# A transformer of two layers with routed experts: the last normalization's rows loaded behind the second nest, and a sixth further weight slot in that layer

## The chip, the core and the metric

The kernel runs on one core of a Trainium2 chip, as one launch. The metric is device microseconds of an execution, as the median of several runs. The profile is of one further execution, with its own time.

## What is computed

256 tokens of width 1024 go through two layers. Layer 0 mixes tokens by attention (with a context of 256 further tokens), layer 1 by a gated long convolution. Behind each mixer stands a normalization, a mixture of 16 experts of which each token takes two, and another normalization. Cut to what matters here:

```
for i in range(2):
    y = attention(...) if i == 0 else hyena(...)
    x = layer_norm(alpha * x + g1 * y, ln_g[i, 0], ln_b[i, 0])
    f = moe_ffn(x * (1 + sc2) + sh2, router_w, router_bias, exp_w_gate[i], exp_w_up[i], exp_w_down[i])
    x = layer_norm(alpha * x + g2 * f, ln_g[i, 1], ln_b[i, 1])
return x
```

`moe_ffn` computes `(silu(t @ w_gate[e]) * (t @ w_up[e])) @ w_down[e]` for each token `t` and each of its two experts `e`, weighted by the router. All is float32. One expert's three matrices are 12 MB, which the kernel loads as 12 tiles of 1 MB: four gate, four up, four down.

## The kernel before

**Weights and slots.** All weights go through tiles named `w` of 128 x 2048 float32 (1 MB), loaded by SP in the order of the program (line 144, in `load`). `ring` has 12 of them (`RING`). In the experts of a layer, `more_ring` opens further slots beside the ring, named w0, w1 and so on: four in layer 0 and five in layer 1 (`MORE = [4, 5]`). `wtile` hands the slots out by turns: the ring's 12, then the further ones, then the ring's again. A load into a slot waits until the last reader of what was in it has ended. SP issues strictly in order, so a load that waits holds up all loads behind it.

**The experts of a layer** are in `moe`. The experts are sorted by their number of tokens and taken by position. Positions 0 to 9 are always computed in blocks of 32 tokens or 64: `up` (line 646, the gate and up products), `turn_mid` (line 655), `down` (line 665), `back` (lines 684 and 690, which adds into `xs`). The two fullest experts are computed densely over all 256 tokens, in eight pieces, one in each of the positions 1 to 8 (`PIECES`): an up piece (`dense_up`, line 709) or a down piece (`dense_down`, line 721), each with four or two of the 1 MB tiles. Positions 10 and up are rarely needed. They stand in a nest of branches (`rare`, line 759), which is entered only if such a position has tokens.

**Around the nest.** Position 9 (`NEST`) is computed behind the nest, but its first loads are issued ahead of it, into the further slots alone: `expert_loads(l, ix, most=MORE[l], new=True)`. `new=True` takes w0, w1 and so on from the start. To this end position 8's down tiles are kept to the ring (`all_slots(0)`). Behind the nest come the rest of position 9's loads:

```
w = expert_loads(l, ix, most=MORE[l], new=True)
last.back()
last = None
rare(RARE)
E.bank = E.banks()
E.w = expert_loads(l, ix, have=w)
```

**The end.** Behind layer 1's experts the last normalization is computed by DVE (`ln_stats`, lines 359 to 365, then lines 1407 and 1408), with `ln_g[1, 1]` and `ln_b[1, 1]` spread over all partitions in a tile `gbf` of 1 MB. `gbf` lies in a pool `gp` of its own, and POOL loads it (line 1399). The order in which each engine's instructions stand is set by a scheduler when the program is built: `gbf`'s loads stand far ahead of the experts, at the start of layer 1's mixer. The result leaves by lines 1410 and 1412.

Two tiles of the dense experts matter to the change: `hid` (128 x 1024, one buffer), which holds the hidden values of a dense piece, and `do` (128 x 512, two buffers), which takes its scaled output (line 723). Both are free once position 8's dense down piece is done, unless the innermost branch of the nest (`beyond`) uses them.

Of the kernel before, what the change touches and what calls it, by code (L numbers as in the profile page):

```python
# [7 lines left out]
F32 = mybir.dt.float32  # L8
# [4 lines left out]
ALU = mybir.AluOpType  # L13
# [5 lines left out]
N, D, NE, FF = 256, 1024, 16, 1024  # L19
# [6 lines left out]
PAD = -3e38  # L26
RING = 12

MORE = [4, 5]


DENSE = 2
# [45 lines left out]
def emit(tc, I, O):  # L78
    nc = tc.nc
    pe, act, dve, pool, sp = nc.tensor, nc.scalar, nc.vector, nc.gpsimd, nc.sync  # L80
    es = ExitStack()

    with es:
# [42 lines left out]
        def all_slots(n):  # L126
            slots["more"] = n
            slots["turn"] = RING + n - 1
# [49 lines left out]
        xs = cp.tile([128, 2, D], F32, name="xs")  # L178
# [169 lines left out]
        def row_bc(pool_, src, tag, eng):  # L348
            t = pool_.tile([128, D], F32, name=tag, tag=tag, bufs=1)
            eng.dma_start(out=t, in_=src.to_broadcast([128, D]))  # L350
            return t

        def mod_bc(pool_, l, v, tag, eng):
            return row_bc(pool_, mdram[l, v].rearrange("a b -> (a b)")[None, :], tag, eng)

        def ln_stats(r, e=0):
            st = sm.tile([128, 2, 6], F32, name="st")
            for hf in range(2):
                dve.bn_stats(st[:, hf, :], r[:, 512 * hf:512 * hf + 512])  # L359
            mv = sm.tile([128, 2], F32, name="mv")  # L360
            dve.bn_aggr(mv, st)  # L361
            sd = sm.tile([128, 1], F32, name="sd")
            act.activation(sd, mv[:, 1:2], AF.Sqrt, bias=epsc[:, e:e + 1])
            rs = sm.tile([128, 1], F32, name="rs")
            dve.reciprocal(rs, sd)  # L365
            return mv, rs
# [37 lines left out]
        def mixer_tail(l, stage, mixT, wout, R):  # L404

            g1b = mod_bc(stage, l, 0, "g1b", sp)
            early = expert_loads(l, 0, most=MORE[l], new=True)
            all_slots(MORE[l])
            ca, cb = fold[:, l, 0], fold[:, l, 1]
# [315 lines left out]

        ENG = [ET.PE, ET.Activation, ET.DVE, ET.Pool, ET.SP]

        def moe(l, h2, R, first, filler):
            with tc.tile_pool(name=f"mp{l}", bufs=2, reuse_waits="tile") as mp:
                g2b = mod_bc(mp, l, 1, "g2b", pool)  # L730
                g2r = mp.tile([128, 256], F32, name="g2r", tag="g2r", bufs=1)
# [7 lines left out]
                def expert(p):  # L739
                    i = place(p)  # L740
                    tab = (R["rank"][:, :, 0:1], R["wt"][:, :, 0:1]) if p == 0 else (R["rankP"][:, :, i:i + 1], R["wtP"][:, :, i:i + 1])
                    return Expert(mp, SLOTS[i], tab, h2, (fold[:, l, 0], fold[:, l, 1]), (g2b, g2r), p == NEST)
# [1 line left out]
                def number(row, i, engines, top):  # L744
                    return nc.values_load(ints[0:1, row, i:i + 1], engines=engines, min_val=0, max_val=top)

                lng = row_bc(mp, I["ln_g"][l, 0:1, :], "hid", pool)
                lnb = [mp.tile([128, 512], F32, name="do", tag="do", bufs=2) for _ in range(2)]
                for hf in range(2):
                    pool.dma_start(out=lnb[hf], in_=I["ln_b"][l, 0:1, 512 * hf:512 * hf + 512].to_broadcast([128, 512]))  # L750
                E = expert(0)
                E.pick(R["weights"])
                with tc.issue_after(E.turn_in()):
                    R["permute"](mp)
                second = expert_loads(l, 1, most=MORE[l])
                def rare(p):


                    with tc.If(number(4, place(p), ENG, N + 1) > 0):  # L759
                        E = expert(p)  # L760
                        E.w = expert_loads(l, number(1, place(p), [ET.SP], NE - 1))
                        E.pick()
                        E.turn_in()
                        E.up()
                        E.weights_in()
                        E.turn_mid()
                        E.down()
                        E.back()
                        if p + 1 < NPOS:
                            rare(p + 1)  # L770
                        else:
                            with tc.If(number(2, 0, ENG, 1) > 0):
                                beyond()
# [28 lines left out]
                hid, last = {}, None  # L802
                for p in range(RARE):
                    if p == NEST:

                        ix = number(1, place(p), [ET.SP], NE - 1)
                        w = expert_loads(l, ix, most=MORE[l], new=True)
                        last.back()
                        last = None
                        rare(RARE)  # L810
                        E.bank = E.banks()
                        E.w = expert_loads(l, ix, have=w)
                    elif p == 0:
                        E.w = first
                    else:
                        ix = number(1, place(p), [ET.SP], NE - 1) if p > 1 else 1
                        E.w = expert_loads(l, ix, have=second if p == 1 else (), most=8)
                        if p in PIECES:
                            r, half, down = PIECES[p]
                            dw = dense_loads(l, number(1, 2 + r, [ET.SP], NE - 1), half, down)  # L820
                        if p + 1 == NEST:
                            all_slots(0)
                        E.w = expert_loads(l, ix, have=E.w)
                    E.up()
                    if last:
                        last.back()
                    nxt = expert(p + 1) if p + 1 < RARE else None
                    if nxt:
                        nxt.pick()
                    if p == 0:  # L830
                        for t in range(2):
                            dve.tensor_tensor(out=xs[:, t, :], in0=h2[:, t, :], in1=lng, op=ALU.mult)
                            for hf in range(2):
                                s_ = slice(512 * hf, 512 * hf + 512)
                                dve.tensor_tensor(out=xs[:, t, s_], in0=xs[:, t, s_], in1=lnb[hf], op=ALU.add)
                    E.turn_mid()
                    if p in PIECES:
                        if down:
                            dense_down(mp, E.bank, dw, hid[r], R["wtP"][:, :, 2 + r:3 + r], g2b)
                        else:  # L840
                            hid[r] = dense_up(mp, E.bank, dw, h2T)
                    if filler:
                        filler(p, E.bank)
                    if nxt:
                        nxt.turn_in()
                    if p != NEST:
                        E.weights_in()
                    E.down()
                    if p + 1 == NEST:
                        nxt.weights_in()  # L850
                    E, last = nxt, E
                last.back()

                act.activation(dumm, epsc[:, 0:1], AF.Sqrt)
                if l == 0:
                    for t in range(2):
                        ln_core(xs[:, t, :], xs[:, t, :], 1)
# [15 lines left out]
        R = routing_tables()  # L873
        mixT = hm([128, KC, N], "mixT")
        with tc.tile_pool(name="s0", bufs=1) as s0:
# [15 lines left out]
            for h in mod_first():  # L891
# [3 lines left out]
                for dc in range(4 * h, 4 * h + 4):  # L895
                    for r in range(2):
# [3 lines left out]
                        else:  # L900
                            dve.tensor_scalar(out=v_, in0=v_, scalar1=scp[:, r, dc:dc + 1], scalar2=mcol(0, 0, r)[:, dc:dc + 1],
                                              op0=ALU.mult, op1=ALU.add)
# [183 lines left out]
            mv = [c_ for l in range(2) for v in range(6) if l or v > 1 for c_ in mod_vec(l, v)]  # L1086
# [30 lines left out]
            for qc in range(2):  # L1117
                sq = tmp()
                pool.tensor_tensor(out=sq, in0=o_sb[:, qc].rearrange("p h d -> p (h d)"),
                                   in1=o_sb[:, qc].rearrange("p h d -> p (h d)"), op=ALU.mult)  # L1120
# [14 lines left out]
        if True:  # L1135
            wo = out_weights(I["attn_w_out"][0])
            rmore = more_ring(0)
            with tc.tile_pool(name="s0b", bufs=1, reuse_waits="tile") as s0b:
                h2, first = mixer_tail(0, s0b, mixT, wo, R)
# [105 lines left out]
        R = routing_tables()  # L1245
        if True:
# [146 lines left out]
            rmore = more_ring(1)  # L1393
            with tc.tile_pool(name="s1b", bufs=1, reuse_waits="tile") as s1b:
                h2, first = mixer_tail(1, s1b, z2T, wo, R)
        gp = es.enter_context(tc.tile_pool(name="gp", bufs=1, reuse_waits="tile", side="right"))
        gbf = gp.tile([128, 2, D], F32, name="gbf")
        for a, nm in enumerate(("ln_g", "ln_b")):
            pool.dma_start(out=gbf[:, a], in_=I[nm][1, 1:2, :].to_broadcast([128, D]))
        moe(1, h2, R, first, None)  # L1400
        ov = O["out"].rearrange("o (t p) d -> p (o t) d", p=128)
        st = [ln_stats(xs[:, t, :], 1) for t in range(2)]
        for t in range(2):
            mv, rs = st[t]
            for hf in range(2):
                s_ = slice(512 * hf, 512 * hf + 512)
                dve.scalar_tensor_tensor(out=xs[:, t, s_], in0=xs[:, t, s_], scalar=mv[:, 0:1], in1=gbf[:, 0, s_], op0=ALU.subtract, op1=ALU.mult)  # L1407
                dve.scalar_tensor_tensor(out=xs[:, t, s_], in0=xs[:, t, s_], scalar=rs, in1=gbf[:, 1, s_], op0=ALU.mult, op1=ALU.add)  # L1408
                if t:
                    (act if hf else sp).dma_start(out=ov[:, t, s_], in_=xs[:, t, s_])  # L1410
            if t == 0:
                sp.dma_start(out=ov[:, t, :], in_=xs[:, t, :])
        less_ring(rmore)


# [57 lines left out]
```

## Time and profile before

| | us |
|---|---|
| median of 3 runs | 1301.54 |
| lowest and highest of them | 1300.76, 1306.81 |
| the profiled execution | 1297.5 |
| its span, first to last instruction | 1295.7 |
| TensorE (PE) busy | 1161.9, 90% of the span |
| VectorE (DVE) busy | 549.3, 42% |
| ScalarE (ACT) busy | 214.9, 17% |
| GpSimd (POOL) busy | 48.8, 4% |
| DMA | 443.87 MB, mean 343 GB/s |
| mean granted TensorE clock | 0.953 of full speed |

Times in the profile are from the span's start. PE is TensorE's matmuls, PEld its weight loads, PEq its sequencer, SPq the instruction stream of SP that issues loads. DMA share is the mean busy share of the core's 16 DMA engines. A float32 matmul stands in the trace as two records. The two nests end at about 720 us (layer 0, whose nest is taken) and 1257 us (layer 1, whose nest is not taken).

### The profile page before, as it was taken

Reading aid. Unit: us, or ns where it says so; the run is one execution under the profiler, and the core shown is the slowest. Engines: PE = TensorE matmul, PEld = TensorE weight load, DVE = VectorE, ACT = ScalarE, POOL = GpSimd, SP = SyncE. Lnnn points to the kernel's source line nnn. Section 1 sums busy time; section 2 is a strip of 40 time slices with the busy share of each in tenths; the row PEclk is TensorE's granted clock in tenths of the full one; section 3 lists DMA queues with packets and bytes.
Section 4 is the critical chain, followed back from the end, with each engine's and each line's share of the span. In section 5 each row is a group of like instructions: output and inputs, shape, how many; then the busy total and the mean of one; then the engine's idle time right before and its main releaser. Section 6 shows DMA issues by size and latency. Waiting matters only on the chain. (4 is left out here: it accounts for less than half of the span.)

```text
span 1295.7 us, 19951 instructions
## 1 busy us (share of the span) xinstructions
PE 1161.9 (90%) x8106; PEld 696.2 (54%) x8106; DVE 549.3 (42%) x1131; ACT 214.9 (17%) x431; POOL 48.8 (4%) x88
## 2 busy tenths in 40 slices
PE   5999989979999989999686779899699999999983
PEld 2345645448437466485443468684374374665741
DVE  2376998461231432414311268993712213223133
ACT  2133646120000000000000044410300000000000
POOL 1000000210000000000200010000100000000000
PEclk9999999989999999999778789999899999999986
DMA  9999894879998998999999784378799999999964
GB/s 325 397 402 349 307 356 180 310 263 406 409 401 340 400 401 329 397 398 363 382 385 395 294 345 177 109 299 316 266 405 408 402 358 396 405 373 401 408 249 196
DMA packets 133206, 443.87 MB, mean 343 GB/s; under 512 B 8271, under 2 KB 9895, under 8 KB 133104
## 3 DMA queue, kind: packets, MB, share of 16 engines
q1 hardware_dynamic: 127168, 426.76, 85.0%
q0 software_dynamic: 4864, 13.18, 3.0%
q10 hardware_dynamic: 1072, 2.54, 0.6%
q8 instruction: 67, 1.10, 0.3%
q14 instruction: 35, 0.29, 0.1%
HBM read 437.19 MB, written 5.26 MB: 341 GB/s over the span
## 5 line engine op out<-in xcount | busy, mean ns | idle before, releaser
L646 PE MATMUL acc<-w,xe 128*32 128x256 f32 (+1 forms) x2688 | 217.6, 430 | 11.4 <-PEq L759 5.9
L709 PE MATMUL acc<-xnT,w 128*128 128x256 f32 x1024 | 222.3, 379 | 0.0
L709 PEld LDWEIGHTS acc<-xnT,w 128*128 128x128 f32 x1024 | 194.4, 190 | 25.6
L646 PEld LDWEIGHTS acc<-w,xe 128*32 128x32 f32 (+1 forms) x2688 | 102.4, 120 | 115.0 <-issue 66.6
L665 PE MATMUL acc<-w,aT 128*32 128x256 f32 (+1 forms) x1344 | 115.5, 420 | 10.2 <-DMA w<-in_exp_w_down 6.0
L721 PE MATMUL acc<-w,hid 128*128 128x512 f32 x256 | 111.4, 593 | 0.3 <-DVE xs L690 0.3
L712 DVE TENSOR_TENSOR hid<-hid,acc 128x256 f32<-128x256 f32 x32 | 13.5, 421 | 197.0 <-ACT hid L711 197.0
L665 PEld LDWEIGHTS acc<-w,aT 128*32 128x32 f32 (+1 forms) x1344 | 47.5, 116 | 63.6 <-issue 27.4
L269 DVE SCALAR_TENSOR_TENSOR w<-w,cz 128x1024 f32<-128x1024 f32 x60 | 75.8, 1289 | 11.4 <-DMA w<-in_mod_w 11.4
L721 PEld LDWEIGHTS acc<-w,hid 128*128 128x128 f32 x256 | 48.1, 190 | 58.1 <-issue 57.3
L690 DVE TENSOR_TENSOR xs<-xs,acc 128x512 f32<-128x512 f32 x92 | 57.4, 682 | 47.5 <-PE acc L684 47.5
L937 PE MATMUL acc<-w,hT 128*128 128x512 f32 (+1 forms) x192 | 71.2, 523 | 0.0
L650 DVE TENSOR_TENSOR ac<-ac,acc 128x256 f32<-128x256 f32 (+1 forms) x23 | 10.7, 467 | 138.3 <-PE acc L646 138.3
L1294 PE MATMUL acc<-hTh,w 128*128 128x256 f32 x320 | 59.9, 286 | 0.0
L723 DVE SCALAR_TENSOR_TENSOR do<-acc,wtP,g2b 128x512 f32<-128x512 f32 x32 | 24.0, 751 | 69.6 <-PE acc L721 69.6
L937 PEld LDWEIGHTS acc<-w,hT 128*128 128x128 f32 x192 | 35.6, 190 | 31.7 <-issue 29.3
L1294 PEld LDWEIGHTS acc<-hTh,w 128*128 128x128 f32 x320 | 49.6, 188 | 2.2 <-ACT ed L1324 1.3
L711 ACT ACTIVATE hid<-acc 128x256 f32<-128x256 f32 x32 | 12.3, 383 | 207.7 <-PE acc L709 207.7
L649 ACT ACTIVATE ac<-acc 128x256 f32<-128x256 f32 (+1 forms) x23 | 9.7, 420 | 217.0 <-PE acc L646 217.0
L614 PE MATMUL mis<-h,Pu 128*32 128x256 f32 (+1 forms) x336 | 33.6, 462 | 13.3 <-DVE Pu L608 8.5
L1294 PE MATMUL acc<-hTl,w 128*128 128x256 f32 x160 | 44.8, 280 | 0.0
L684 PE MATMUL acc<-xg,PT 32*128 32x256 f32 (+1 forms) x336 | 39.9, 441 | 4.1 <-DVE xg L670 3.8
(351 smaller groups left out, 1264.9 us busy)
## 6 DMA issues: line engine op xcount, KB each, us to landing
w<-in_exp_w_gate SPq DMA_DIRECT2D x108, 1024.0 KB, 17.5
w<-in_exp_w_up SPq DMA_DIRECT2D x108, 1024.0 KB, 17.4
w<-in_exp_w_down SPq DMA_DIRECT2D x108, 1024.0 KB, 14.2
w<-in_mod_w SPq DMA_DIRECT2D x40, 1024.0 KB, 9.0
w<-in_hy_w_in SPq DMA_DIRECT2D x12, 1024.0 KB, 19.5
w<-in_attn_w_in SPq DMA_DIRECT2D x9, 1024.0 KB, 11.2
w<-in_mod_w SPq DMA_DIRECT2D x16, 512.0 KB, 10.8
w<-in_attn_w_out SPq DMA_DIRECT2D x4, 1024.0 KB, 11.7
```

Of the source, the lines that this page charges most:

```text
L269: dve.scalar_tensor_tensor(out=st["acc"][:, k], in0=w[:, k], scalar=c_[k], in1=st["acc"][:, k], op0=ALU.mult, op1=ALU.add)
L614: pe.matmul(gb[S * j:S * j + S, 0:nn], Pu[:, t, 0:S], self.h2[:, t, nn * j:nn * j + nn], start=(t == 0), stop=(t == 1), tile_position=(0, ...
L646: pe.matmul(A[m][S * j:S * j + S, 0:nn], self.xe[:, kc, :], w[:, nn * j:nn * j + nn], tile_position=(0, S * j), start=(kc == 0), stop=(kc ...
L665: pe.matmul(y[S * q:S * q + S, 0:nn], lhs, w[:, nn * q:nn * q + nn], tile_position=(0, S * q), start=(kc == 0), stop=(kc == KC - 1))
L684: pe.matmul(o, self.PT[r, 128 * t:128 * t + 128], self.yb[r, 0:nn], start=True, stop=True, tile_position=(S * q, 0))
L690: dve.tensor_tensor(out=x_, in0=x_, in1=o, op=ALU.add)
L709: pe.matmul(b[:, N * m:N * m + N], ws[m][kc // 4][:, kc % 4, 128 * fb:128 * fb + 128], h2T[:, kc, :], start=(kc == 0), stop=(kc == KC - 1))
L712: dve.tensor_tensor(out=hid[:, fb, :], in0=hid[:, fb, :], in1=b[:, N:2 * N], op=ALU.mult)
L721: pe.matmul(b, hid[:, fb, 128 * t:128 * t + 128], ws[fb // 2][:, fb % 2, s_], start=(fb == 0), stop=(fb == 3))
L723: dve.scalar_tensor_tensor(out=o, in0=b, scalar=wt[:, t], in1=g2b[:, s_], op0=ALU.mult, op1=ALU.mult)
L937: pe.matmul(bank[:, 0:width], hT[:, kc, 128 * t:128 * t + 128], st["w"][kc // per][:, kc % per, :], start=(kc == 0), stop=(kc == KC - 1))
L1294: pe.matmul(b[:, 0:N], w_, m, start=(kc == 0 and i == 0), stop=(kc == KC - 1 and i == len(ps) - 1))
```

## The change

The pool `gp` with `gbf` is taken out. `ln_g[1, 1]` is loaded into a tile `hid` and the two halves of `ln_b[1, 1]` into two tiles `do`, by POOL, behind the nest of layer 1 (`norm_rows`, through the new argument `fin` of `moe`). The last normalization moves into a function `store`, called at the end of `moe`. The 8 KB of each partition that `gbf` took go to a sixth further slot in layer 1 (`MORE = [4, 6]`): the ring turns over 18 slots there instead of 17, and six of position 9's loads are issued ahead of the nest instead of five.

```diff
-MORE = [4, 5]
+MORE = [4, 6]
...
-        def moe(l, h2, R, first, filler):
+        def store(gf, bf):
+
+            ov = O["out"].rearrange("o (t p) d -> p (o t) d", p=128)
+            st = [ln_stats(xs[:, t, :], 1) for t in range(2)]
+            for t in range(2):
+                mv, rs = st[t]
+                for hf in range(2):
+                    s_ = slice(512 * hf, 512 * hf + 512)
+                    dve.scalar_tensor_tensor(out=xs[:, t, s_], in0=xs[:, t, s_], scalar=mv[:, 0:1], in1=gf[:, s_], op0=ALU.subtract, op1=ALU.mult)
+                    dve.scalar_tensor_tensor(out=xs[:, t, s_], in0=xs[:, t, s_], scalar=rs, in1=bf[hf], op0=ALU.mult, op1=ALU.add)
...
+        def norm_rows(mp, l, i):
+            g = row_bc(mp, I["ln_g"][l, i:i + 1, :], "hid", pool)
+            b = [mp.tile([128, 512], F32, name="do", tag="do", bufs=2) for _ in range(2)]
+            for hf in range(2):
+                pool.dma_start(out=b[hf], in_=I["ln_b"][l, i:i + 1, 512 * hf:512 * hf + 512].to_broadcast([128, 512]))
+            return g, b
+
+        def moe(l, h2, R, first, filler, fin=None):
...
-                lng = row_bc(mp, I["ln_g"][l, 0:1, :], "hid", pool)
-                lnb = [mp.tile([128, 512], F32, name="do", tag="do", bufs=2) for _ in range(2)]
-                for hf in range(2):
-                    pool.dma_start(out=lnb[hf], in_=I["ln_b"][l, 0:1, 512 * hf:512 * hf + 512].to_broadcast([128, 512]))
+                lng, lnb = norm_rows(mp, l, 0)
...
                         rare(RARE)
+                        if fin:
+                            rows = norm_rows(mp, l, 1)
                         E.bank = E.banks()
                         E.w = expert_loads(l, ix, have=w)
...
                 act.activation(dumm, epsc[:, 0:1], AF.Sqrt)
+                if fin:
+                    fin(*rows)
...
-        gp = es.enter_context(tc.tile_pool(name="gp", bufs=1, reuse_waits="tile", side="right"))
-        gbf = gp.tile([128, 2, D], F32, name="gbf")
-        for a, nm in enumerate(("ln_g", "ln_b")):
-            pool.dma_start(out=gbf[:, a], in_=I[nm][1, 1:2, :].to_broadcast([128, D]))
-        moe(1, h2, R, first, None)
...
+        moe(1, h2, R, first, None, store)
```

Three places of the built program show what moves. The first is SP's stream ahead of layer 1's nest, with the semaphores that a row waits for in brackets (DMAHW0 to DMAHW7 are SP's DMA semaphores, PE is TensorE's). Before, w0 to w4 are position 9's early loads, each waiting for TensorE, and the last row shown is the branch that ends the nest:

```order
L144 DMA w_8618<-in_exp_w_down 128x2x1024 [waits DMAHW5_49,PE_49]
...
L144 DMA w0_8806<-in_exp_w_gate 128x2x1024 [waits DMAHW6_49,PE_49]
...
L144 DMA w1_8808<-in_exp_w_up 128x2x1024 [waits DMAHW7_49,PE_49]
...
L144 DMA w4_8814<-in_exp_w_gate 128x2x1024 [waits DMAHW2_49,PE_49]
L745 TENSOR_LOAD ints_5445 [waits DVE_49]
...
L759 UNCONDITIONAL_BRANCH [waits SP_sequencer_49,DMAHW0_49,DMAHW1_49,DMAHW2_49,DMAHW3_49,DMAHW4_49,DMAHW5_49,DMAHW6_49,DMAHW7_49] x4
```

With the change:

```order
L144 DMA w0_8602<-in_exp_w_down 128x2x1024 [waits DMAHW0_49,PE_49]
...
L144 DMA w1_8604<-in_exp_w_down 128x2x1024 [waits DMAHW1_49,PE_49]
...
L144 DMA w0_8800<-in_exp_w_gate 128x2x1024 [waits DMAHW6_49,DMAHW0_49,PE_49]
...
L144 DMA w1_8802<-in_exp_w_up 128x2x1024 [waits DMAHW7_49,DMAHW1_49,PE_49]
...
L144 DMA w2_8804<-in_exp_w_gate 128x2x1024
...
L144 DMA w5_8810<-in_exp_w_up 128x2x1024 [waits DMAHW3_49]
L767 TENSOR_LOAD ints_5445 [waits DVE_49]
...
L778 UNCONDITIONAL_BRANCH [waits SP_sequencer_49,DMAHW0_49,DMAHW1_49,DMAHW2_49,DMAHW3_49,DMAHW4_49,DMAHW5_49,DMAHW6_49,DMAHW7_49] x4
```

Position 8's dense down tiles now lie in w0 and w1 (the first two rows), the early loads are six, those of w2 to w5 wait for no instruction of TensorE, and the branch waits for the same semaphores as before.

The second place is TensorE in position 8, where the last up products (line 646) are followed by the dense down piece (line 721; `acc` are its banks). Before, w0 to w4 are read by line 646 and the dense down piece reads two tiles of the ring:

```order
L646 MATMUL acc1_8429<-w4_8592,xe_8531 32x256 x8
L646 MATMUL acc0_8428<-w_8594,xe_8531 32x256 x8
L646 MATMUL acc1_8429<-w_8596,xe_8531 32x256 x8
L655 MATMUL acc0_8428<-blob_72,ac_8684 128x128 x2
L721 MATMUL acc4_8432<-w_8608,hid_8456 128x512 x2
L721 MATMUL acc5_8433<-w_8608,hid_8456 128x512 x2
```

With the change:

```order
L655 MATMUL acc0_8422<-blob_72,ac_8678 128x128 x2
L721 MATMUL acc4_8426<-w0_8602,hid_8450 128x512 x2
L721 MATMUL acc5_8427<-w0_8602,hid_8450 128x512 x2
L721 MATMUL acc4_8426<-w1_8604,hid_8450 128x512 x2
L721 MATMUL acc5_8427<-w1_8604,hid_8450 128x512 x2
L721 MATMUL acc4_8426<-w0_8602,hid_8450 128x512 x2
L721 MATMUL acc4_8426<-w1_8604,hid_8450 128x512 x2
L721 MATMUL acc5_8427<-w0_8602,hid_8450 128x512 x2
L721 MATMUL acc5_8427<-w1_8604,hid_8450 128x512 x2
L665 MATMUL acc2_8424<-w_8606,aT_8713 32x256 x8
```

The last readers of w0 and w1 ahead of the nest are now the last four matmuls of the dense down piece.

The third place is POOL from the end of layer 1's nest to the end of the program, as a difference:

```order
-L759 UNCONDITIONAL_BRANCH x4
-L1469 UNCONDITIONAL_BRANCH
...
+L778 UNCONDITIONAL_BRANCH x4
+L350 DMA hid<-in_ln_g 128x1024
+L747 DMA do<-in_ln_b 128x512 x2
+L1476 UNCONDITIONAL_BRANCH
```

POOL now issues three loads behind the nest, where it had nothing left to do.

## Rows read from the trace of the kernel before

**Rows 1.** The chain that ended last, its end: start us, us, what

```profile
1260.62 17.64 DMA w<-in_exp_w_down
1278.26 0.04 issue
1278.31 1.92 PE acc L665 x16
...
1291.68 0.75 DVE xs L1408
```

**Rows 2.** Timeline of SP, 1205 to 1296: start us, us, what it issues

```profile
1203.94 16.38 SPq L144 DMA_DIRECT2D w<-in_exp_w_down  x6
1224.26 0.38 SPq L144 DMA_DIRECT2D w<-in_exp_w_gate  x1
...
1231.65 0.37 SPq L144 DMA_DIRECT2D w<-in_exp_w_gate  x1
1256.60 0.39 SPq L144 DMA_DIRECT2D w<-in_exp_w_up  x1
...
1258.92 2.08 SPq L144 DMA_DIRECT2D w<-in_exp_w_down  x4
```

**Rows 3.** Timeline of PE, 1205 to 1296: start us, us, what [idle before <-releaser]

```profile
1222.29 2.77 PE L646 MATMUL acc<-w,xe 128*32 128x256 f32 x48
...
1234.20 13.90 PE L721 MATMUL acc<-w,hid 128*128 128x512 f32 x32
1248.03 3.66 PE L665 MATMUL acc<-w,aT 128*32 128x256 f32 x64
1252.24 1.15 PE L684 MATMUL acc<-xg,PT 32*128 32x256 f32 x16 [0.55 <-DVE xg L670]
1256.92 9.18 PE L646 MATMUL acc<-w,xe 128*32 128x256 f32 x112 [3.53 <-PEq L759]
```

**Rows 4.** Busy time by stretch of 4 us: engines, PEclk, DMA share, GB/s

```profile
1208.00:1212.00 4.00, 4.00 (x20) 3.54 (x19) 0.00 (x0) 0.00 (x0) 0.00 (x0) 1.00 1.02 409
...
1244.00:1248.00 4.00, 4.00 (x10) 1.52 (x8) 1.44 (x2) 0.00 (x0) 0.00 (x0) 1.00 0.41 163
1248.00:1252.00 4.00, 3.69 (x65) 1.98 (x64) 1.68 (x3) 0.00 (x0) 0.00 (x0) 1.00 0.00 0
1252.00:1256.00 4.00, 1.15 (x16) 0.72 (x16) 2.67 (x5) 0.00 (x0) 0.00 (x0) 1.00 0.03 6
1256.00:1260.00 4.00, 3.08 (x32) 1.69 (x36) 0.00 (x0) 0.00 (x0) 0.00 (x0) 0.51 0.55 167
```

**Rows 5.** SP's waits, 1200 to 1296: us in total, times, longest us

```profile
SPq L759 <- SPq L759: 14.5, 4, 5.2
SPq L144 <- PEq L759: 8.7, 1, 8.7
```

**Rows 6.** Waits of all engines for others, 925 to 1256: total, times, longest

```profile
PEld acc L646 <- DMA w<-in_exp_w_gate: 0.3, 1, 0.3
```

**Rows 7.** DMA issues: count, KB each, median us from issue to landing

```profile
hid<-in_ln_g POOLq DMA_DIRECT2D x2, 512.0 KB, 4.5
do<-in_ln_b POOLq DMA_DIRECT2D x4, 256.0 KB, 4.6
gbf<-in_ln_g POOLq DMA_DIRECT2D x1, 512.0 KB, 9.0
gbf<-in_ln_b POOLq DMA_DIRECT2D x1, 512.0 KB, 10.5
```

**Rows 8.** Timeline of POOL, 715 to 775

```profile
747.52 0.55 POOL L1399 DMA_DIRECT2D gbf<-in_ln_g  x1
748.07 0.55 POOL L1399 DMA_DIRECT2D gbf<-in_ln_b  x1
```

**Rows 9.** Timelines of ACT, DVE and PE, 730 to 790, one row of each

```profile
758.81 0.46 ACT L383 ACTIVATE hT<-mis,fold 128x128 f32<-128x128 f32 x1 [2.25 <-DMA w<-in_hy_w_in]
...
758.32 0.41 DVE L385 TENSOR_SCALAR hT<-mis,fold 128x128 f32<-128x128 f32 x1 [0.29 <-PE mis L379]
...
757.16 1.97 PE L379 MATMUL mis<-blob,xs 128*128 128x128 f32 x8 [6.13 <-DVE xs L373]
```

**Rows 10.** SP's waits, 690 to 725 (the nest of layer 0)

```profile
SPq L759 <- SPq L759: 15.1, 2, 9.8
```

More of the change, by code (lines that the diff above doesn't have):

```diff
@@ L726, in emit @@
         ENG = [ET.PE, ET.Activation, ET.DVE, ET.Pool, ET.SP]
-        def moe(l, h2, R, first, filler):
+        def store(gf, bf):
[7 more added lines that the diff above has]
+                    dve.scalar_tensor_tensor(out=xs[:, t, s_], in0=xs[:, t, s_], scalar=rs, in1=bf[hf], op0=ALU.mult, op1=ALU.add)
+                    if t:
+                        (act if hf else sp).dma_start(out=ov[:, t, s_], in_=xs[:, t, s_])
+                if t == 0:
+                    sp.dma_start(out=ov[:, t, :], in_=xs[:, t, :])
+        def norm_rows(mp, l, i):
[5 more added lines that the diff above has]
+        def moe(l, h2, R, first, filler, fin=None):
             with tc.tile_pool(name=f"mp{l}", bufs=2, reuse_waits="tile") as mp:
@@ L1395, in emit @@
                 h2, first = mixer_tail(1, s1b, z2T, wo, R)
-        gp = es.enter_context(tc.tile_pool(name="gp", bufs=1, reuse_waits="tile", side="right"))
-        gbf = gp.tile([128, 2, D], F32, name="gbf")
-        for a, nm in enumerate(("ln_g", "ln_b")):
-            pool.dma_start(out=gbf[:, a], in_=I[nm][1, 1:2, :].to_broadcast([128, D]))
-        moe(1, h2, R, first, None)
[L1401 to L1412, printed above, removed]
+        moe(1, h2, R, first, None, store)
         less_ring(rmore)
```

## Prediction

> **What bounds the kernel now.** I read the chain that ended last first: it names what set the end. Its last steps are the load of the last down matrix, 17.64 us from issue to landing at 1278.26, then 17.4 us of tail (matmuls of that load, the add into xs, the last normalization, the store) [rows 1]. So the end is set by when SP's last expert load lands, not by TensorE, busy as it is over the span. Second, SP's own issues [rows 2]: five loads between 1224.26 and 1231.65 go into the further slots w0 to w4 (the early loads of the expert behind the nest), then nothing until 1256.60, when the other seven follow. Third, the DMA share by stretch [rows 4]: the engines are full until the early loads are in, idle from about 1246 to 1258, then full again. That idle stretch is SP standing at the nest. Fourth, SP's waits [rows 5]: 14.5 us at line 759 in four pieces, then 8.7 us for TensorE's sequencer at the same line. The first order rows of the change show what line 759's branch waits for on SP: every one of its eight DMA semaphores, so SP leaves the nest only when all its loads have landed. The four pieces are the landings of the early loads. In layer 0, whose nest is taken, SP again stands 15.1 us at that line [rows 10].
>
> TensorE before that point is full: the dense down piece runs from 1234.20 to 1248.10, then the position's own down, then the way back; it comes out of the nest at 1256.92 [rows 3]. From 925 to 1256 its weight loads wait for DMA three times for 0.3 us (one of the three in [rows 6]). Layer 1's experts are therefore bound by TensorE, and weights that come earlier there buy nothing.
>
> **The change, part by part.**
>
> *Loads into gbf go.* 1 MB leaves POOL's queue at 747.5 [rows 8], where the engines were full. What waited for DMA there is one ACT instruction: it starts at 758.81, its twin on DVE, freed by the same transposes, at 758.32 [rows 9]. Gain: between nothing and 0.5 us. I take 0.2, since TensorE goes on without a gap from 757.16.
>
> *A sixth slot inside the layer.* Prefetch becomes 1 MB deeper. With 0.9 us of DMA waits in 330 us [rows 6], I cost it at nothing; the cover is TensorE's own work.
>
> *The slots turn.* This is the term that decides. With 18 slots instead of 17, position 8's weights fall elsewhere. Before, w0 to w4 were read last by position 8's up products, which lets the early loads go while line 646 runs: w0 at 1224.26, within the stretch of 48 matmul records from 1222.29 [rows 2, 3]. Now w0 and w1 hold the two halves of the dense down piece, and of its last four matmuls two still read w0 and two w1. The 32 records of that piece take 13.90 us, 0.434 each, two to a matmul [rows 3]; w1's last two matmuls are four records, 1.74 us. So w0 comes free at 1248.10 - 1.74 = 1246.4 instead of 1224.3, w1 at 1248.1. The loads of w2 to w5 need not wait for TensorE, but they stand behind these two in SP's queue. SP then comes to the nest some 20 us late, and its branch waits for six fresh loads.
>
> One load is 1.049 MB; at 409 GB/s [rows 4] that is 2.56 us. The seven loads behind the nest took from 1256.60 to 1278.26, 21.66 us [rows 1, 2], so a burst costs 3.7 us once (issue, start, landing) beside 2.56 each.
>
> *ln_g and ln_b behind the nest.* 1 MB on POOL, in three issues of about 0.55 us as gbf's [rows 8]. POOL has nothing outstanding and leaves the nest with the other engines near 1256.6 [rows 2, 3], while SP still stands there; so this MB goes into the middle of SP's six. The two gbf loads landed after 9.0 and 10.5 us beside a full SP queue, against 4.5 for the same size in a quieter place [rows 7]: queues share the engines. I add it as one more load, 2.56 us. Bounds: nothing, if it lands in the gap behind the six; twice that, 5.1, if half-size rows are slow (256 KB of ln_b took 4.6 us, as long as 512 KB of ln_g [rows 7]). DVE needs the rows only in the tail, long after. The tail has the same instructions.
>
> *The sum.* First burst: 1246.4 + 3.7 + 7 x 2.56 = 1268.0; TensorE has left the nest and its products follow the landings. SP goes on, six loads: 1268.0 + 3.7 + 6 x 2.56 = 1287.1. Before: 1278.26. Later by 8.8, less 0.2: **8.6 us slower**. The profiled execution took 1297.5 us (span 1295.7), so it becomes 1306.1. The runs shown lie above it: the lowest by 3.3, the median by 4.0; I take 3.7 and forecast **1309.8 us**.
>
> The rate is where a page and the trace part. The rows show 409 GB/s for 4 us on end and the like in the stretches around. The Trainium skill, "DMA: Bandwidth & Descriptors", section "Bandwidth", puts what HBM gives one core at about 358 GB/s; by that a load would be 2.93 us and the sum 13.4 us. The measurement decides, and 358 gets no chance.
>
> **The rivals.**
>
> 1. *POOL's MB costs nothing.* It lands while SP passes from one burst to the next. First burst 1246.4 + 3.7 + 6 x 2.56 = 1265.5, second 1284.6: 6.3, less 0.2, so 6.1 slower, 1307.3 us. For it: the gap of 3.7 us would hold 2.56. Against it: gbf's slow landing beside SP's loads [rows 7]. The Trainium skill, same page, section "Queues, rings and completion order", has each DMA engine go round its queues packet by packet; by that rule this rival would fail, and the sum stands at 8.6.
>
> 2. *SP is not held for its loads.* If the pieces at line 759 are something else, SP goes on at 1256.6 and all thirteen MB run in one burst: 1246.4 + 3.7 + 13 x 2.56 = 1283.4, 5.1 later, less 0.2: 4.9 slower, 1306.1 us. For it: the profile names SP itself as the releaser, not a DMA [rows 5]. Against it: the semaphores in the order rows, and that the last piece ends as the engines run dry [rows 4].
>
> 3. *The other side: the sixth early load fills the idle stretch.* If the six are in before the nest ends, six instead of seven remain: 1256.6 + 3.7 + 6 x 2.56 = 1275.7, 2.6 earlier, and 0.2: 2.8 faster, 1298.4 us (with POOL's MB among them, no change). It decides at 1256.6 - 3.7 - 15.4 = 1237.5: w0 must be free by then. For it: 11 us of idle engines [rows 4]. Against it: w0's last reader ends at 1246.4, nine later, behind a full TensorE [rows 3].
>
> 4. *The change does not do what it says:* the rows of ln_g and ln_b could hold the end if they came late. POOL issues them near 1257 and DVE wants them 30 us later; no chance worth naming.
>
> **How the numbers follow.** Forecast 0.68 (up to 11.2 slower with POOL's MB at twice its price, 1312.4), rival 1 0.12, rival 2 0.15, rival 3 0.04, the rest 0.01. The range takes in rivals 1 and 2 and the dear end, with about one us for the spread of the runs: 1305 to 1313; rival 3 stays out. About 0.5% (6.5 us) is what a measurement of this kernel can tell from no change. Slower by over that, above 1308.0: the forecast but for a tenth of it, and a little of rival 1: 0.64. Rivals 1, 2 and 3 lie within: 0.34. Faster: 0.02.
>
> **What would show it.** In the changed profile SP should issue w0 near 1246 and w5 near 1251, with the DMA share near zero from about 1233 to 1248; SP should wait at the nest's branch (line 778 there) until about 1268, then issue six loads, the last landing near 1287; TensorE's last 16 matmuls of line 665 follow it, and the tail is again 17.4 us. POOL's three loads start near 1257. At 750 to 1230 nothing should differ by over 1 us. I am wrong if w0 is issued before 1240, if SP's next load comes at 1257, or if POOL's loads land only after SP's burst.

## Result and the profile after

| | before | changed |
|---|---|---|
| median us | 1301.15 | 1310.62 |
| lowest to highest us | 1299.12 to 1306.81 (4 runs) | 1309.88 to 1311.1 (4 runs) |
| ratio of the runs, 95% interval | | 1.007, [1.0049, 1.009] |
| span of the profiled execution, us | 1295.7 | 1308.9 |

The change makes the kernel 9.1 us slower (0.007 of 1301.15; 6.4 to 11.7 by the interval). The forecast was 1309.8, with 1305 to 1313 as its range.

The two profiled executions differ by 13.2 us, more than the runs do, because the one of before was quick for its kernel (1297.5 where the median is 1301.15). Where that comes from is read at one mark that both have, the begin of position 8's dense down piece (line 721). Up to there the changed execution is 4.54 us behind: 1.24 of it are there within the first 75 us, and 4.75 when layer 0's experts end (TensorE's line 684 there at 754.64 against 749.89), all in code that the change does not touch. This distance differs from one execution to the next: in the five experiments below the mark lies anywhere from 1235.26 to 1241.68. So stretches are told from that mark on below: to the end of the span it is 61.5 us before and 70.2 changed, 8.7 more.

The chain that ended last, its end (start us, us, what), answering to [rows 1]:

```profile
1276.16 16.04 DMA w<-in_exp_w_down
1292.21 0.04 issue
1292.25 1.11 PE acc L665 x16
...
1304.82 0.75 DVE xs L737
```

The same shape: the last down matrix lands, at 1292.2, and 16.7 us of tail follow (17.4 before). Told from the mark, the landing is 9.4 us later than before (53.5 against 44.1), and the tail 0.7 shorter. The timeline of SP, answering to [rows 2]:

```profile
1204.85 22.59 SPq L144 DMA_DIRECT2D w<-in_exp_w_down  x6
1250.95 0.37 SPq L144 DMA_DIRECT2D w<-in_exp_w_gate  x1
1252.67 0.37 SPq L144 DMA_DIRECT2D w<-in_exp_w_up  x1
...
1254.95 0.37 SPq L144 DMA_DIRECT2D w<-in_exp_w_up  x1
1273.05 0.39 SPq L144 DMA_DIRECT2D w<-in_exp_w_gate  x1
...
1274.39 2.15 SPq L144 DMA_DIRECT2D w<-in_exp_w_down  x4
```

The first early load goes at 1250.95, 12.2 us after the mark, where before it went 9.9 us ahead of it. The second waits until 1252.67, and four follow at once. Then SP issues nothing until 1273.05. The timeline of TensorE, answering to [rows 3]:

```profile
1238.74 13.90 PE L721 MATMUL acc<-w,hid 128*128 128x512 f32 x32
1252.57 3.66 PE L665 MATMUL acc<-w,aT 128*32 128x256 f32 x64
1256.78 1.15 PE L684 MATMUL acc<-xg,PT 32*128 32x256 f32 x16 [0.55 <-DVE xg L670]
1263.68 5.90 PE L646 MATMUL acc<-w,xe 128*32 128x256 f32 x72 [5.75 <-PEq L778]
```

The dense down piece is as long as before, ends at 1252.64, and w0 is reloaded 1.69 us ahead of that end, w1 at it. SP's waits from 1215 to 1312 (us in total, times, longest), answering to [rows 5], and its DMA by stretch, answering to [rows 4]:

```profile
SPq L144 <- PE acc L721: 23.8, 2, 22.7
SPq L778 <- SPq L778: 16.4, 5, 5.7
```

```profile
1236.00:1240.00 4.00, 3.38 (x41) 1.70 (x34) 0.64 (x2) 0.77 (x2) 0.00 (x0) 1.00 0.12 45
1240.00:1244.00 4.00, 4.00 (x11) 1.82 (x10) 0.00 (x0) 0.00 (x0) 0.00 (x0) 1.00 0.01 2
1244.00:1248.00 4.00, 4.00 (x11) 1.79 (x10) 2.88 (x4) 0.00 (x0) 0.00 (x0) 1.00 0.00 0
1248.00:1252.00 4.00, 4.00 (x10) 1.71 (x9) 1.44 (x2) 0.00 (x0) 0.00 (x0) 1.00 0.01 2
1256.00:1260.00 4.00, 1.38 (x22) 0.72 (x16) 2.48 (x5) 0.00 (x0) 0.00 (x0) 1.00 1.01 388
1268.00:1272.00 4.00, 1.58 (x32) 0.68 (x23) 0.00 (x0) 0.00 (x0) 0.00 (x0) 1.00 0.82 322
1272.00:1276.00 4.00, 1.50 (x24) 0.68 (x24) 0.00 (x0) 0.00 (x0) 0.00 (x0) 1.00 0.48 128
```

A wait that did not exist before, 22.7 us for the dense down piece, stands ahead of the nest, and the 16.4 us at the branch (line 778 now) end late. Before, the 14.5 us there were over before TensorE reached the end of the nest, and SP then waited 8.7 us for TensorE's sequencer [rows 5]; now SP issues its next load 9.4 us after TensorE has begun its first product behind the nest (1273.05 against 1263.68). The DMA engines are nearly idle from about 1237 to 1252, while TensorE computes, and idle again near 1273, where one burst has ended and the next has not begun.

### The profile page after: what moved, and what is told of

Same layout as the page of the kernel before. It is cut to its first block, busy times and chain, and to the rows that moved or that the text cites. A ratio compares the mean times of both kernels' runs of the same rounds, so it can differ in the third digit from the quotient of the medians.

```text
span 1308.9 us, 19955 instructions
## 1 busy us (share of the span) xinstructions
PE 1162.0 (89%) x8106; PEld 694.1 (53%) x8106; DVE 549.5 (42%) x1131; ACT 214.8 (16%) x431; POOL 49.5 (4%) x89
## 5 line engine op out<-in xcount | busy, mean ns | idle before, releaser
L712 DVE TENSOR_TENSOR hid<-hid,acc 128x256 f32<-128x256 f32 x32 | 13.4, 420 | 197.1 <-ACT hid L711 197.1
```

The source lines that it names most:

```text
L712: dve.tensor_tensor(out=hid[:, fb, :], in0=hid[:, fb, :], in1=b[:, N:2 * N], op=ALU.mult)
```

## The experiments

All are small edits of the changed kernel and leave none of the work out. A burst is told by SP's first load behind the nest and the landing of the last down matrix at the end of the chain; these times are of one profiled execution of each kernel.

| | ratio to before, 95% interval | mark, line 721 | SP's first load behind the nest | last landing | burst | mark to end of span |
|---|---|---|---|---|---|---|
| before | 1 | 1234.20 | 1256.60 | 1278.26 | 21.7 | 61.5 |
| changed | 1.007 [1.0049, 1.009] | 1238.74 | 1273.05 | 1292.21 | 19.2 | 70.2 |
| dense tiles in the ring | 0.9991 [0.9976, 1.0005] | 1235.26 | 1257.54 | 1279.53 | 22.0 | 61.8 |
| rows alone | 1.0013 [0.9999, 1.0027] | 1235.56 | 1258.06 | 1282.51 | 24.5 | 63.6 |
| rows behind the loads | 1.0047 [1.0031, 1.0063] | 1238.85 | 1270.78 | 1290.00 | 19.2 | 68.3 |
| both | 0.9973 [0.9956, 0.9989] | 1241.68 | 1263.89 | 1283.19 | 19.3 | 59.7 |
| slots in another order | 0.9994 [0.998, 1.0008] | 1236.69 | 1258.83 | 1281.14 | 22.3 | 62.9 |

### Undo the slots' turn: the dense down tiles in the ring

```diff
+                        if l and p + 1 == NEST:
+                            all_slots(0)
                         if p in PIECES:
                             r, half, down = PIECES[p]
                             dw = dense_loads(l, number(1, 2 + r, [ET.SP], NE - 1), half, down)
-                        if p + 1 == NEST:
+                        if not l and p + 1 == NEST:
                             all_slots(0)
```

> The changed kernel, with the two dense down tiles of position 8 in layer 1 kept to the ring, so that w0 to w5 are free when the early loads are issued; all else as changed. If the loss comes from w0 and w1 being read by the dense down piece: all six early loads are issued before TensorE begins that piece (about 10 us or more before it ends, against at its end), are in when TensorE leaves the nest, SP leaves the nest with TensorE, and six loads of SP and 1 MB of POOL then run as long as seven loads did, 21.7 us: time as before the change or 0.2 us under it, about 1301. If the loss comes from the rows loaded behind the nest or from the deeper ring as such: it stays, 1308 to 1311. If POOL's MB costs nothing: 1298.

Measured: 1300.48 us beside 1301.63, ratio 0.9991, no difference from before that the runs can tell. The timeline of SP in this kernel, two rows of its waits, and the chain's last load:

```profile
1226.67 0.53 SPq L144 DMA_DIRECT2D w<-in_exp_w_gate  x1
...
1235.66 4.09 SPq L144 DMA_DIRECT2D w<-in_exp_w_up  x1
1257.54 0.39 SPq L144 DMA_DIRECT2D w<-in_exp_w_gate  x1
```

```profile
SPq L778 <- SPq L778: 14.9, 5, 5.1
SPq L144 <- PEq L778: 1.6, 1, 1.6
```

```profile
1260.70 18.83 DMA w<-in_exp_w_down
```

All six early loads are issued by about the mark (1235.26), SP has its loads in before TensorE leaves the nest and waits 1.6 us for it; it issues its next load 22.3 us behind the mark (22.4 before, 34.3 changed), and the burst, now six loads and POOL's MB, takes 22.0 us (21.7 for seven loads). Keeping two tiles out of w0 and w1 takes the whole loss away. The burst also shows that the rows behind the nest cost what the sixth slot gives, to within 0.3 us.

### The price of POOL's MB: the rows alone, and the rows behind the loads

The first is the change with `MORE = [4, 5]`. In the second, `norm_rows` takes the engine as an argument:

```diff
                         rare(RARE)
-                        if fin:
-                            rows = norm_rows(mp, l, 1)
                         E.bank = E.banks()
                         E.w = expert_loads(l, ix, have=w)
+                        if fin:
+                            rows = norm_rows(mp, l, 1, sp)
```

> The change without the sixth slot: five further slots as before, ln_g and ln_b loaded by POOL behind the nest. Early loads are issued as before the change. If POOL's MB takes its share of the DMA engines from SP's burst of seven loads: last landing 24.2 us after SP's first load behind the nest instead of 21.7, 2.6 us longer, less 0.2 for the loads into gbf: about 1303.6. If POOL's MB costs nothing: 1301. If the slots were not the cause and the rows were: near 1310.

> The changed kernel with one difference: ln_g and ln_b are issued by SP behind the last expert load instead of by POOL at the end of the nest. The early loads still wait for the dense down piece. If POOL's MB lengthens the first burst: SP is held at the nest 2.6 us less (last early load lands 19 us after the first is issued, against 21.5), last expert load lands 2.6 us earlier: about 1308. If it costs nothing: 1310.6, as changed.

Measured: rows alone 1.0013, which is 1.7 us (from nothing to 3.5): the runs cannot quite part the 2.4 expected (2.6 less 0.2) from nothing. The bursts of the traces can, as the three bursts of six loads without POOL's MB are within 0.14 us of each other (19.16, 19.22 and 19.30). With the rows alone, seven loads behind the nest take 24.5 us instead of 21.7. The chain's last load there and SP's first load behind the nest:

```profile
1262.44 20.07 DMA w<-in_exp_w_down
```

```profile
1258.06 0.39 SPq L144 DMA_DIRECT2D w<-in_exp_w_up  x1
```

With the rows behind the loads, 1.0047 against 1.007 as changed, 3.0 us less by the middles (the intervals overlap). SP's timeline of it:

```profile
1251.07 0.38 SPq L144 DMA_DIRECT2D w<-in_exp_w_gate  x1
...
1270.78 0.39 SPq L144 DMA_DIRECT2D w<-in_exp_w_gate  x1
...
1274.45 0.66 SPq L350 DMA_DIRECT2D hid<-in_ln_g  x1
```

The chain's last load there:

```profile
1273.90 16.10 DMA w<-in_exp_w_down
```

From the first early load to the first load behind the nest it is 19.7 us here and 22.1 in the changed kernel, 2.4 us apart. With the rows alone POOL's MB costs 2.8 us (24.5 against 21.7), with the dense tiles in the ring 2.8 (22.0 against 19.2), and in the last experiment below, the slots in another order, 3.1 (22.3 against 19.2). So it costs about what one more load of SP does, 2.4 to 3.1 us in four places against the 2.56 estimated for a load.

### Both: a version under either kernel

> Both: the dense down tiles of position 8 in the ring, and ln_g and ln_b issued by SP behind the last expert load. Six loads instead of seven behind the nest and nothing beside them: last landing 19.1 us after SP's first load there, 2.6 us less than before the change, and 0.2 for the loads into gbf: about 1298.4, under the kernel before. The rows land some 2.6 us behind the last weights, ahead of their first use. If the idle DMA engines ahead of the nest are worth nothing, or the rows come too late for DVE: 1301 or more.

Measured: ratio 0.9973, [0.9956, 0.9989], 3.5 us under before (1.4 to 5.7); the medians, 1299.6 beside 1301.63, lie 2.0 apart. Its profiled execution was a late one up to the mark and is the quickest from there, 59.7 us: the last landing comes 2.6 us earlier than before, told from the mark, and a tail of 18.2 us instead of 17.4 takes 0.8 of it back. The chain's last load, and SP's timeline:

```profile
1267.27 15.92 DMA w<-in_exp_w_down
```

```profile
1263.89 0.39 SPq L144 DMA_DIRECT2D w<-in_exp_w_gate  x1
...
1267.83 0.60 SPq L350 DMA_DIRECT2D hid<-in_ln_g  x1
```

Six loads stand behind the nest, 19.3 us, and the rows come behind them; the last normalization does not wait for them, since the chain goes from the last load through the products to it. What the change set out to do with the slot works, once the slot is free in time and the rows stay out of the burst.

### Only the order in the queue: the same slots, the free ones first

```diff
-                ts.append(load(src(nm, i), [2, 1024], slot=len(ts) if new else None))
+                ts.append(load(src(nm, i), [2, 1024], slot=((len(ts) + 2) % 6 if l and not isinstance(idx, int) else len(ts)) if new else None))
```

> The changed kernel with one difference: position 9's six early loads go into w2, w3, w4, w5, w0, w1, in this order, so that the two that wait for the dense down piece stand last in SP's queue. If the price is that loads which need not wait stand behind two that must, and that SP then waits for their landing: four loads are issued ahead of the dense down piece, two at its end (12.2 and 13.9 us after it begins), these are in 21 us after it begins, SP leaves the nest about with TensorE at 22 to 24, six loads and POOL's MB take 21.7 us, and from the dense down piece's begin to the end it is 61 to 62 us, as before the change (61.5) against 70.2 as changed: about 1301. If SP were not held for its loads, or if any load that waits for that piece cost the same: 1306 to 1310.

Measured: 0.9994, no difference from before; from the mark to the end 62.9 us, 0.9 above the 61 to 62 expected; the tail there is 18.5 us, 1.0 longer than before. SP's timeline and the chain's last load:

```profile
1228.77 1.29 SPq L144 DMA_DIRECT2D w<-in_exp_w_up  x1
1248.91 0.37 SPq L144 DMA_DIRECT2D w<-in_exp_w_gate  x1
1250.62 0.37 SPq L144 DMA_DIRECT2D w<-in_exp_w_up  x1
1258.83 0.39 SPq L144 DMA_DIRECT2D w<-in_exp_w_gate  x1
```

```profile
1262.63 18.51 DMA w<-in_exp_w_down
```

Its waits show that the two late loads still stood for the dense down piece, 18.6 and 1.1 us, that SP waited once at the branch, and that it then waited 1.2 us for TensorE's sequencer:

```profile
SPq L144 <- PE acc L721: 19.7, 2, 18.6
SPq L778 <- SPq L778: 5.0, 1, 5.0
SPq L144 <- PEq L778: 1.2, 1, 1.2
```

The slots are the same and w0 and w1 are reloaded at the same places, 12.2 and 13.9 us behind the mark, yet the loss is gone. What costs is therefore not the waiting slot by itself, but the four loads that stand behind it in an ordered queue and then delay the branch.

## Why the prediction was right

*What bounds the kernel.* Right: the chain of the changed kernel ends in the same load and tail, and in all five experiments the end moved with the last landing. The tail was not as steady as the forecast had it: 16.7 to 18.5 us.

*The slots turn.* Right in place and size. Told from the mark, w0 was to go at 12.2 us and went at 12.2, w1 at 13.9 and went at 13.9; SP was to leave the nest at 33.8 and issued its next load at 34.3; the last load was to land at 52.9 and landed at 53.5 (12.2 and 13.9 are 1246.4 and 1248.1 less 1234.2; 33.8 and 52.9 are 1268.0 and 1287.1 less that). That the whole came out so close, 8.7 us from the mark to the end against 8.6, is in part luck: the landing was 0.6 us later than forecast, 0.5 of it in the first burst, and a tail 0.7 us shorter than the 17.4 forecast made up for it. Two experiments that free the queue, by the slots or by their order, take the whole loss away.

*POOL's MB.* Right in size, 2.4 to 3.1 us against the 2.56 taken, but not in its start: POOL left the nest 24.9 us behind the mark, not 22.8. POOL's timeline:

```profile
1263.62 0.54 POOL L350 DMA_DIRECT2D hid<-in_ln_g  x1 [343.72 <-PEq L778]
1264.15 1.07 POOL L747 DMA_DIRECT2D do<-in_ln_b  x2
```

It still fell into SP's first burst, so the sum did not feel it. Rival 1 (the MB costs nothing) falls by the traces of the rows alone and of the rows behind the loads; the two bounds of this term, nothing and 5.1 us, were both away from it.

*The loads into gbf.* No run shows the gain of 0.2 us, and the step named for it did not happen. From the last line 684 of layer 0 to the mark it is 484.31 us before and 484.10 changed, 0.2 less; but in the five experiments, which are without these loads too, the same stretch takes 484.14, 484.56, 484.12, 485.28 and 485.14 (in the order of the table), in three of them more than before. So it scatters by more than the term. The ACT instruction that was to start earlier [rows 9] did not: by its timeline and DVE's it again begins half a microsecond behind its twin, after the same idle time of 2.25 us, and is again put down to a DMA:

```profile
763.57 0.46 ACT L383 ACTIVATE hT<-mis,fold 128x128 f32<-128x128 f32 x1 [2.25 <-DMA w<-spec]
```

```profile
763.08 0.41 DVE L385 TENSOR_SCALAR hT<-mis,fold 128x128 f32<-128x128 f32 x1 [0.29 <-PE mis L379]
```

The term was too small to matter to the forecast.

*The sixth slot inside the layer.* Right: costed at nothing, and the changed kernel's distance to before stays within 0.1 us from 926 to the mark (4.54 to 4.58 us behind).

*The rate.* The rows of 409 GB/s settle it, but the price that the prediction puts on the other rate, 13.4 us, does not follow: it keeps the 3.7 us that were worked out with 2.56 us for a load. With 2.93 us for each, seven loads in 21.66 us leave 1.15 us, and the same sum gives 8.3 us. Nor do the page and the trace part there: the same section of the Trainium skill, "DMA: Bandwidth & Descriptors", "Bandwidth", gives 358 GB/s as a core's share when both cores of a domain stream, and 425 GB/s as measured with one core alone, and this kernel runs on one core.

*Rival 2* (SP is not held for its loads) falls. SP's last wait at line 778 ends between 1272.0 and 1272.7, as the first burst runs dry, and its next load follows; with the rows taken out of the burst that load comes 2.4 us earlier after the first one. *Rival 3*, the idle stretch filled by the sixth load, is what the version with both edits does: with w0 free it gives 3.5 us (1.4 to 5.7) against the 2.8 forecast for that case.

## What to carry to other kernels

A ring that turns over more slots changes which load waits for which reader, in places far from the edit: follow each early load to the last reader of its slot before counting the slot as a gain. In an ordered queue, put the loads that need not wait first, and ask what a branch behind the queue waits for. A load that is moved to an idle engine's queue still takes its time from the DMA engines; put it behind what the end waits for.

## What the runs showed that was not expected

Leaving the nest of layer 1 took TensorE longer in the two executions in which the DMA engines were full. The idle time ahead of its first matmul behind that nest, put down to its own sequencer at the branch, was 3.27 to 3.64 us in the five executions in which the DMA share in the 3.4 us ahead was 0.03 to 0.05 (before among them, [rows 3]), and 5.75 and 6.10 us in the two in which it was 1.02: the changed kernel, and the rows behind the loads, whose row of TensorE's timeline is this:

```profile
1264.13 5.76 PE L646 MATMUL acc<-w,xe 128*32 128x256 f32 x72 [6.10 <-PEq L778]
```

Beside it the kernel with the slots in another order:

```profile
1259.15 7.51 PE L646 MATMUL acc<-w,xe 128*32 128x256 f32 x104 [3.27 <-PEq L778]
```

The Trainium skill, "Runtime: NRT & Kernel Launch", section "Instruction fetch mechanics", says that a taken branch outside the fetched window fetches its target by DMA before it goes on; the DMA queues of the profile include two for instructions, and both moved packets in these stretches, which fits. The cause stays open: no run here separates that fetch, and the two executions are also the only ones in which SP still stood at the branch. The longer exit cost nothing in these two kernels, since the last landing that SP waited for came later than TensorE's exit. In the kernel before SP waited for TensorE's sequencer [rows 5], so there a longer exit would have moved SP's burst.

The tail is not fixed either: its last 16 matmuls of line 665 took 1.07 us or 1.74 to 1.93, and those of line 684 took 1.15 or 2.09. The quick ones ran at a granted clock of 1.00, which is 2.4 GHz; of the slow ones, those of 1.93 and 2.09 us ran at 0.50, which is 1.2 GHz, and the two of 1.74 and 1.86 us at 0.59 and 0.55 on the mean. In every one of these bursts TensorE had worked in pieces of at most 9.2 us between waits; which wait brings the clock down was not pursued. So tails of the same products ran from 16.7 to 18.5 us.
